# The first expert pair's rows: one-hot matrix held stationary, token rows streamed 512 columns at a time

## The chip, the cores and the metric

The kernel runs on one core of a Trainium2 chip, in one launch. The metric is device time in microseconds (us). Before the change, three runs gave 748.46, 750.91 and 753.99 us; the median is 750.91 us. Lower is better. The trace comes from one further, profiled execution of the same kernel.

## The reference

The reference is one decoder layer on 512 tokens of 1024 float32 values. Only its second half matters here, a hierarchical mixture of experts:

```python
hn2 = rms_norm(h, ffn_norm_g[l]).reshape(Bsz * S, D)
...
g_idx = jnp.argmax(p_group, axis=-1)                      # one of 4 groups per token
top_vals, top_idx = lax.top_k(logits_sel, TOP_K)          # two of its 8 experts
...
act = jax.nn.silu(hg) * hu * comb[:, g, :, None]
y = y + jnp.einsum('tef,efd->td', act, w_down[g])
```

In the first half the layer does a short gated convolution, a differential attention and an output projection; the sum of these and the input is `h`. Every token then goes to 2 of 32 experts, each a SwiGLU network with two matrices of 1024x512 (gate, up) and one of 512x1024 (down), all float32. The reference computes every expert for every token and weights most of them with zero.

## The kernel before, in words

**Stages.** The kernel works through the input projection, convolution and attention, the output projection together with the routing, and then the experts two by two (16 pairs). The tensor `y` holds h in SBUF: 128 partitions (tokens) by 4 chunks by 1024 columns. Each expert has 64 slots, so that a pair fills 128 rows. Tokens beyond 64 for one expert are left to a loop at the end (`overflow`).

**Rows of a pair.** For every later pair q the kernel makes a one-hot matrix of tokens by slots (`prepare`, L939), gets the token number of each slot by a small product (`index`, tile `pi`, L948), and fetches the rows with an indirect DMA from a copy of h in DRAM (`hrow`) to the SBUF tile `xr`. `turned` (L996 and on) then turns these rows: eight TensorE transposes of 128x128 into two PSUM banks of four each (tile `pxt2`, L1003), which ScalarE (L1009, one bank, four instructions) and VectorE (L1006, the other bank, one instruction) scale by the norm's gain `gf` and write to `xt`. Each `xt[:, k]` is a stationary operand of the gate and up products (`gate_up`, L1018 and L1019); column k of eight is every eighth value of a row.

**Rows of the first pair.** For pair 0 no DMA is used. `first_slots` makes its one-hot matrix `oh0` chunk by chunk (L853), once `place` (L834) has the positions of the chunk's tokens. `first_rows(c, h)` (L856 to L862) then multiplies: for each of four k, 128 columns of `y` (every eighth one) are the stationary operand and `oh0[:, c]` is the moving one, so that the result comes out already turned, in PSUM tile `px[h]`. It accumulates over the four chunks c. `first_turned` (L980 to L986) scales `px[0]` with VectorE (L983) and `px[1]` with ScalarE (L985) into `xt`. The trace has two matmul records for each float32 product, so 4 chunks x 2 halves x 4 products are 64 records on L861.

**Order.** The schedule is by hand: each engine executes in the order in which the program issues. Around the change, TensorE's order is: output projection of chunk 3 (`po`), `first_rows(0, 0)`, transposes of chunk 3 for the router (`pht`, L688), positions of chunk 1 (`ppos`, L831), `first_rows(0, 1)`, router of chunk 3 (`pr`, L695), positions of chunk 2, `first_rows(1, 0)`, `(1, 1)`, `(2, 0)`, positions of chunk 3, `first_rows(2, 1)`, `(3, 0)`, `(3, 1)`, the index products of pair 1 (`pi`), the counts, and then the gate and up products of expert 0 (`pgu`). VectorE runs the router's selection of each chunk (`route`, L796 to L822, ending in `ohm`) between these. After expert 0's products TensorE gets the gates of pair 0 by a product (`pcw`, L991), which needs `comb`, the end of a chain of small VectorE and ScalarE instructions (`gates`).

**Weights.** SP's queue issues the expert weights in a fixed order (L740) into a ring of 8 tiles of 2 MB (`we`) and one of 4 tiles of 1 MB (`wm`); a load waits until the tile it overwrites has been used. ScalarE's queue writes `hrow` and the gates `crow` to DRAM; GpSimd's queue issues the indirect fetches into `xr` and `cw`.

**Memory.** `xr` has one buffer. Before the change it is first filled with zeros by GpSimd (L1146); pair 1's fetch then writes to it.

Of the kernel before, what the change touches and what calls it, by code (L numbers as in the profile page):

```python
# [8 lines left out]
F32 = mybir.dt.float32  # L9
# [4 lines left out]
AF = mybir.ActivationFunctionType  # L14
OP = mybir.AluOpType
AX = mybir.AxisListType

P = 128
D = 1024
S = 512  # L20
NT = S // P
KD = D // P
# [17 lines left out]
def layer(ctx: ExitStack, tc: tile.TileContext, x, attn_norm_g, w_in, conv_w, conv_out_g,  # L40
# [3 lines left out]
    V, A, T = nc.vector, nc.scalar, nc.tensor  # L44
# [8 lines left out]
    def bank(tag, name, shape=(P, 512)):  # L53
        return psum.tile(list(shape), F32, name=name, tag=tag, bufs=BANKS[tag])
# [4 lines left out]
    def bc(ap, n):  # L59
        return ap.to_broadcast(n)  # L60
# [62 lines left out]
    y = cons.tile([P, NT, D], F32, name="y")  # L123
    xr = x[0].rearrange("(c p) d -> p c d", p=P)
# [10 lines left out]
    G = nc.gpsimd  # L135
# [7 lines left out]
    gf = cons.tile([P, KD], F32, name="gf")  # L143
# [629 lines left out]
    def rtt(name, *shape, dt=F32, bufs=1):  # L773
        return rt.tile([P] + list(shape), dt, name=name, bufs=bufs)
# [74 lines left out]
    oh0 = rtt("oh0", NT, 2, SLOTS)  # L849
    px = []  # L850
# [4 lines left out]

    def first_rows(c, h):  # L856
        if len(px) == h:
            px.append(bank("S", "px", (P, 4, P)))
        for j in range(4):
            k = 4 * h + j  # L860
            T.matmul(px[h][:, j], y[:, c].rearrange("p (q k) -> p k q", k=KD)[:, k], oh0[:, c].rearrange("p n s -> p (n s)"),  # L861
                     start=(c == 0 and j == 0), stop=(c == NT - 1 and j == 3), skip_group_check=True)  # L862

    def placed(c):
        positions(c)
# [4 lines left out]
    for c in range(NT):  # L870
        out_rest(c, (5,))
        if c:
            router(c - 1, 1)
            advance(tails[c - 1], 4)
        out_rest(c, (6, 7))
        h_add(c, 1, ob[1][c])
        if c < NT - 1:
            out_rest(c + 1, (4,))
        else:
            first_rows(0, 0)  # L880
        h_transposed(c, 1)
        A.dma_start(hrow[c * P:(c + 1) * P, :], y[:, c])
        if c > 1:
            placed(c - 2)
        if c:
            advance(tails[c - 1], 50)
    first_rows(0, 1)
    router(NT - 1, 1)
    placed(NT - 2)
    advance(tails[3], 50)  # L890
    first_rows(1, 0)
    first_rows(1, 1)
    first_rows(2, 0)
# [6 lines left out]
    moe = ctx.enter_context(tc.tile_pool(name="moe", bufs=1, reuse_waits="tile"))  # L900
# [69 lines left out]
    def prepare(q, tag="X"):  # L970

        oh = one_hot(posm[:, :, 2 * q:2 * q + 2], 2)

        def rest():
            i = index(oh, vcol[:, q:q + 1], tag)
            rows[q], cws[q] = fetch(i, P)
            return lambda: fetch_gates(cws[q], i, P)
        return rest

    def first_turned():  # L980

        xt = moe.tile([P, KD, P], F32, name="xt", tag="xt")
        V.tensor_tensor(xt[:, 0:4], px[0], bc(gf[:, 0:4, None], [P, 4, P]), op=OP.mult)  # L983
        for j in range(4):
            A.activation(xt[:, 4 + j], px[1][:, j], AF.Copy, scale=gf[:, 4 + j:5 + j])  # L985
        return xt  # L986

    def first_gates():
        p = pcw
        for c in range(NT):  # L990
            T.matmul(p, oh0[:, c].rearrange("p n s -> p (n s)"), comb[:, c], start=(c == 0), stop=(c == NT - 1))  # L991
        cws[0] = moe.tile([P, NE + 2], F32, name="cw", tag="cw", bufs=3)
        V.tensor_copy(cws[0], p)
        V.tensor_copy(vcol[:, 0:1], p[:, NE + 1:])

    def turned(x, m, tag="X"):  # L996

        xt = moe.tile([P, KD, P], F32, name="xt", tag="xt")
        x = x.rearrange("s (q k) -> s k q", k=KD)
        for k2 in range(2):  # L1000
            p = bank(tag, "pxt2", (P, 4, P))
            for j in range(4):
                T.transpose(p[:, j, 0:m], x[0:m, 4 * k2 + j], idf[0:m, 0:m])  # L1003
            if k2:
                ks = slice(4 * k2, 4 * k2 + 4)
                V.tensor_tensor(xt[:, ks, 0:m], p[:, :, 0:m], bc(gf[:, ks, None], [P, 4, m]), op=OP.mult)  # L1006
            else:
                for j in range(4):
                    A.activation(xt[:, j, 0:m], p[:, j, 0:m], AF.Copy, scale=gf[:, j:j + 1])  # L1009
        return xt  # L1010

    def gate_up(wg, wu, x, h, p, between=None):
# [91 lines left out]
    def overflow(inc, n):  # L1104

        with tc.For_i(0, n, 1):
# [25 lines left out]
            V.tensor_mul(le[0:SLOTS], le[0:SLOTS], cw[0:SLOTS, 0:NE])  # L1132
            V.tensor_reduce(wcol[0:SLOTS], le[0:SLOTS], axis=AX.X, op=OP.add)
            xt = turned(x, SLOTS)
            p = bank("G", "pgu")
            gate_up(w[0], w[1], xt, 0, p)
# [6 lines left out]
                    combine(s, *r, SLOTS, c, cs)  # L1143
            nc.sync.dma_start(oc, y)

    G.memset(moe.tile([P, D], F32, name="xr", tag="xr"), 0.0)  # L1146
    for _ in range(3):
        G.memset(moe.tile([P, NE + 2], F32, name="cw", tag="cw", bufs=3), 0.0)
    xts = {0: first_turned()}
    rest = prepare(1, "T")  # L1150
    fetch1 = rest()
    for cc in range(NT):
# [37 lines left out]
    for q in range(PAIRS):  # L1190
        if q:
            aT = down_t(acts.pop(q - 1), P)
        expert(2 * q)
        if q + 2 < PAIRS:
            rest = prepare(q + 2)
        if q:
            down_pair(q - 1, aT)
        if q == LAST:
            expert(2 * q + 1, lambda: combine_all(q - 1))
        else:  # L1200
            expert(2 * q + 1)
        if q < LAST:
            xts[q + 1] = turned(rows.pop(q + 1), P)
        if q + 2 < PAIRS:
            rest()()
        if 0 < q < LAST:
            combine_all(q - 1)
        if q == 2:
            rt_cm.__exit__(None, None, None)
            lp = ctx.enter_context(tc.tile_pool(name="lp", bufs=1, side="right", reuse_waits="tile"))  # L1210
            nt = lp.tile([P, NE], F32, name="nt")
            inc = lp.tile([P, 2, NE], F32, name="inc")
            tot = lp.tile([P, 1], I32, name="tot")
            it = lp.tile([P, 1], F32, name="it")
            inc = overflow_count()
        if q == 4:
            more = nc.values_load(tot[0:1, 0:1], min_val=0, max_val=NE)
# [57 lines left out]
```

## Time and profile before

| what | value |
|---|---|
| runs | 748.46, 750.91, 753.99 us |
| profiled execution, its own time | 753.25 us |
| its span | 751.5 us |
| mean granted TensorE clock | 0.987 of full speed |
| PE (matmul) busy | 696.5 us, 93% of the span |
| PEld (weight load) busy | 397.6 us, 53% |
| DVE (VectorE) busy | 317.1 us, 42% |
| ACT (ScalarE) busy | 192.8 us, 26% |
| POOL (GpSimd) busy | 73.7 us, 10% |
| DMA moved | 229.41 MB, mean 305 GB/s |

The span is the time from the first to the last instruction of the profiled execution; its own time is 1.75 us longer. Busy shares are means over stages that differ. The page also has a row of DMA throughput in 40 equal slices: it lies near 425 GB/s from about 225 us to 715 us, with one low slice of 290 GB/s at 282 to 300 us. A wait for several things is put down to the one that came last.

### The profile page before, as it was taken

The numbers are of one execution on the slowest core, as the hardware profiler recorded it, in microseconds if no ns is written. First come the engines' busy times: TensorE is split into PE (matmuls) and PEld (weight loads), VectorE is DVE, ScalarE is ACT, GpSimd is POOL, SyncE is SP. The second block draws the span as 40 slices with busy tenths as digits, with TensorE's granted clock in tenths as the row PEclk, the third lists the DMA queues.
The fourth block names the chain that finished last, engine by engine and source line by source line (L and its number), as shares of the span: only waits on it lengthen the run. The fifth ranks groups of instructions, "written<-read, shape, count | busy, mean of one in ns | idle before, by whom it ended". The sixth has DMA issues, their size and how long they took to land.

```text
span 751.5 us, 8843 instructions
## 1 busy us (share of the span) xinstructions
PE 696.5 (93%) x3356; PEld 397.6 (53%) x3356; DVE 317.1 (42%) x646; ACT 192.8 (26%) x409; POOL 73.7 (10%) x100
## 2 busy tenths in 40 slices
PE   6998999999899999999999989998898998997984
PEld 4786778777778783434434424434344343342432
DVE  2465767776642552235414414414132242331332
ACT  2555545554334211111111111111111111110111
POOL 5021300211110011001101101101001010010001
PEclk9999999999999999999999999999998999999998
DMA  8231221122229997999999999999999999999963
GB/s 267 62 108 56 85 57 57 56 58 66 73 70 422 420 413 290 421 428 418 426 421 426 425 420 427 426 423 422 423 427 428 417 424 430 421 425 423 416 220 114
DMA packets 45933, 229.41 MB, mean 305 GB/s; under 512 B 5156, under 2 KB 22822, under 8 KB 31041
## 3 DMA queue, kind: packets, MB, share of 16 engines
q1 hardware_dynamic: 41072, 221.79, 72.7%
q0 software_dynamic: 3136, 4.35, 1.8%
q10 hardware_dynamic: 1680, 2.69, 1.0%
q8 instruction: 27, 0.44, 0.2%
q14 instruction: 18, 0.14, 0.1%
HBM read 228.63 MB, written 4.26 MB: 310 GB/s over the span
## 4 chain that ended last, share of the span: by engine, by line
PE 42%; DMA 34%; issue 11%; DVE 7%; ACT 3%; POOL 2%; SPq 0%; POOLq 0%; ACTq 0%
DMA we<-in_w_exp_gate_dram 11%; DMA we<-in_w_exp_down_dram 9%; PE pgu L1018 7%; DMA wm<-in_w_exp_gate_dram 5%; DMA we<-in_w_exp_up_dram 5%; PE pgu L1019 5%; DMA wm<-in_w_exp_up_dram 4%; PE pdn L1042 4%; PE pq L118 3%; PE pq L119 3%; PE pq L117 3%; PE px L861 2%; PE po L117 1%; PE po L119 1%; PE po L118 1%
## 5 line engine op out<-in xcount | busy, mean ns | idle before, releaser
L1019 PE MATMUL pgu<-we,xt 128*64 128x512 f32 x400 | 181.2, 606 | 17.1 <-DMA we<-in_w_exp_up_dram 17.1
L1018 PE MATMUL pgu<-we,xt 128*64 128x512 f32 x400 | 182.5, 606 | 0.3 <-DMA we<-in_w_exp_gate_dram 0.3
L1025 DVE SCALAR_TENSOR_TENSOR act<-act,cw,pgu 64x512 f32<-64x512 f32 x32 | 23.9, 747 | 213.6 <-ACT act L1024 213.6
L1042 PE MATMUL pdn<-we,aT 128*64 128x512 f32 x384 | 90.6, 594 | 5.8 <-DMA we<-in_w_exp_down_dram 5.8
L1019 PEld LDWEIGHTS pgu<-we,xt 128*64 128x64 f32 x400 | 53.9, 139 | 75.0 <-issue 50.7
L1018 PEld LDWEIGHTS pgu<-we,xt 128*64 128x64 f32 x400 | 53.8, 139 | 58.8 <-issue 56.1
L1024 ACT ACTIVATE act<-pgu,cw 64x512 f32<-64x512 f32 x32 | 21.9, 683 | 234.0 <-PE pgu L1019 190.4
L1080 DVE TENSOR_TENSOR y<-y,pcb 128x512 f32<-128x512 f32 (+1 forms) x129 | 76.9, 666 | 4.2 <-PE pcb L1077 4.0
L1042 PEld LDWEIGHTS pdn<-we,aT 128*64 128x64 f32 x384 | 28.6, 137 | 65.8 <-issue 54.6
L1060 DVE TENSOR_TENSOR rl<-pdn,rh 128x512 fp32r<-128x512 f32 (+1 forms) x33 | 22.3, 675 | 84.8 <-ACT rh L1059 83.1
L1076 PE MATMUL pcb<-rh,sel 128*128 128x512 f32 (+1 forms) x132 | 51.9, 395 | 0.0
L1077 PE MATMUL pcb<-rl,sel 128*128 128x512 f32 (+1 forms) x132 | 50.4, 384 | 0.0
L1019 PE MATMUL pgu<-wm,xt 128*64 128x512 f32 x112 | 49.5, 595 | 0.8 <-DMA wm<-in_w_exp_up_dram 0.8
L1018 PE MATMUL pgu<-wm,xt 128*64 128x512 f32 x112 | 49.8, 595 | 0.2 <-DVE vcol L951 0.2
L961 POOL DMA_INDIRECT xr<-hrow,idx x15 | 15.1, 1006 | 349.1 <-DVE vcol L951 336.9
L109 DVE TENSOR_TENSOR wlo<-raw,whi 128x1024 fp32r<-128x1024 f32 x30 | 37.7, 1255 | 22.7 <-ACT whi L102 22.7
L1059 ACT ACTIVATE rh<-pdn 128x512 fp32r<-128x512 f32 (+1 forms) x33 | 19.3, 584 | 101.5 <-PE pdn L1042 94.4
L117 PE MATMUL pq<-whi,xh 128*128 128x512 f32 x96 | 41.0, 427 | 3.5 <-ACT whi L102 2.0
L117 PE MATMUL pcv<-xh,whi 128*128 128x512 f32 x96 | 41.8, 435 | 0.0
L118 PE MATMUL pq<-wlo,xh 128*128 128x512 f32 x96 | 39.0, 406 | 0.5 <-DVE wlo L109 0.5
L119 PE MATMUL pq<-whi,xl 128*128 128x512 f32 x96 | 39.0, 406 | 0.0
L119 PE MATMUL pcv<-xh,wlo 128*128 128x512 f32 x96 | 38.1, 397 | 0.0
(243 smaller groups left out, 1023.1 us busy)
## 6 DMA issues: line engine op xcount, KB each, us to landing
we<-in_w_exp_gate_dram SPq DMA_DIRECT2D x24, 2048.0 KB, 19.3
we<-in_w_exp_up_dram SPq DMA_DIRECT2D x24, 2048.0 KB, 31.0
we<-in_w_exp_down_dram SPq DMA_DIRECT2D x24, 2048.0 KB, 33.3
wm<-in_w_exp_gate_dram SPq DMA_DIRECT2D x14, 1024.0 KB, 27.6
wm<-in_w_exp_up_dram SPq DMA_DIRECT2D x14, 1024.0 KB
raw<-in_w_in_dram SPq DMA_DIRECT2D x24, 512.0 KB, 3.7
wm<-in_w_exp_down_dram SPq DMA_DIRECT2D x12, 1024.0 KB, 33.5
raw<-in_w_out_dram SPq DMA_DIRECT2D x8, 512.0 KB, 3.6
```

The costliest lines, as they stand in the source:

```text
L109: V.tensor_sub(los[i], raws.pop(i), his[i].bitcast(F32))
L117: T.matmul(o, lh, rh, start=start, stop=False)
L118: T.matmul(o, lh, rl, start=False, stop=False)
L119: T.matmul(o, ll, rh, start=False, stop=stop)
L1018: T.matmul(p[HS[1 - h]], l, wg[k], start=(k == 0), stop=(k == KD - 1))
L1019: T.matmul(p[HS[h]], l, wu[k], start=(k == 0), stop=(k == KD - 1))
L1025: V.scalar_tensor_tensor(a, a, w, p[HS[h]], op0=OP.mult, op1=OP.mult)
L1042: T.matmul(p[hf][HS[h]], aT[:, c, HS[h]], ws2[h][c][:, HALF[hf]], start=(c == 0), stop=(c == 3))
L1060: V.tensor_sub(r[1][0:m, cs], p[0:m], r[0][0:m, cs].bitcast(F32))
L1076: T.matmul(p, s[0:m, ts], rh[0:m, cs], start=True, stop=False)
L1077: T.matmul(p, s[0:m, ts], rl[0:m, cs], start=False, stop=True)
L1080: V.tensor_add(ys, ys, p)
```

## The change

`first_rows` has the operands exchanged: `oh0[:, c]` (128 columns) is stationary and 512 contiguous columns of `y` move, so one product replaces four. The result `px[h]` is then rows by columns, not turned. So it is copied to `xr` (one half by ScalarE, one by VectorE), and the function `turned` that every later pair uses turns it, with PSUM banks of tag K and with the roles of the two engines exchanged (`on_scalar=1`: VectorE scales columns 0 to 3, ScalarE 4 to 7, as `first_turned` did). `first_turned` and the filling of `xr` with zeros go.

```diff
     def first_rows(c, h):
         if len(px) == h:
-            px.append(bank("S", "px", (P, 4, P)))
-        for j in range(4):
-            k = 4 * h + j
-            T.matmul(px[h][:, j], y[:, c].rearrange("p (q k) -> p k q", k=KD)[:, k], oh0[:, c].rearrange("p n s -> p (n s)"),
-                     start=(c == 0 and j == 0), stop=(c == NT - 1 and j == 3), skip_group_check=True)
+            px.append(bank("S", "px"))
+        T.matmul(px[h], oh0[:, c].rearrange("p n s -> p (n s)"), y[:, c, 512 * h:512 * h + 512],
+                 start=(c == 0), stop=(c == NT - 1))
...
-    def first_turned():
-
-        xt = moe.tile([P, KD, P], F32, name="xt", tag="xt")
-        V.tensor_tensor(xt[:, 0:4], px[0], bc(gf[:, 0:4, None], [P, 4, P]), op=OP.mult)
-        for j in range(4):
-            A.activation(xt[:, 4 + j], px[1][:, j], AF.Copy, scale=gf[:, 4 + j:5 + j])
-        return xt
...
-    def turned(x, m, tag="X"):
+    def turned(x, m, tag="X", on_scalar=0):
...
-            if k2:
+            if k2 != on_scalar:
                 ks = slice(4 * k2, 4 * k2 + 4)
                 V.tensor_tensor(xt[:, ks, 0:m], p[:, :, 0:m], bc(gf[:, ks, None], [P, 4, m]), op=OP.mult)
             else:
                 for j in range(4):
-                    A.activation(xt[:, j, 0:m], p[:, j, 0:m], AF.Copy, scale=gf[:, j:j + 1])
+                    k = 4 * k2 + j
+                    A.activation(xt[:, k, 0:m], p[:, j, 0:m], AF.Copy, scale=gf[:, k:k + 1])
...
-    G.memset(moe.tile([P, D], F32, name="xr", tag="xr"), 0.0)
     for _ in range(3):
         G.memset(moe.tile([P, NE + 2], F32, name="cw", tag="cw", bufs=3), 0.0)
-    xts = {0: first_turned()}
+    xr = moe.tile([P, D], F32, name="xr", tag="xr")
+    A.activation(xr[:, 0:512], px[0], AF.Copy)
+    V.tensor_copy(xr[:, 512:D], px[1])
+    xts = {0: turned(xr, P, "K", 1)}
```

## Rows read from the trace of the kernel before

**Rows 1.** Busy time by stretch: PE, PEld, DVE, ACT, POOL; clock, DMA share, GB/s

```profile
224.00:280.00 56.00, 54.79 (x294) 46.15 (x294) 24.58 (x88) 14.62 (x33) 2.27 (x5) 1.00 1.00 417
280.00:285.00 5.00, 5.00 (x26) 1.50 (x22) 2.35 (x16) 1.59 (x3) 0.00 (x0) 1.00 0.73 221
...
293.00:299.00 6.00, 5.57 (x34) 2.90 (x34) 1.58 (x4) 2.42 (x6) 1.49 (x2) 1.00 0.46 129
299.00:715.00 416.00, 392.18 (x1840) 167.36 (x1836) 136.55 (x258) 61.97 (x129) 27.47 (x28) 0.99 1.01 423
```

**Rows 2.** Timeline of SP's queue: start, duration, engine, line, load

```profile
258.52 0.85 SPq L740 DMA_DIRECT2D wm<-in_w_exp_up_dram  x2
...
281.83 0.81 SPq L740 DMA_DIRECT2D wm<-in_w_exp_gate_dram  x2
...
296.49 0.80 SPq L740 DMA_DIRECT2D we<-in_w_exp_down_dram  x2
```

**Rows 3.** Waits of SP's queue, 281 to 284 and 290 to 300: total, times, longest

```profile
SPq L740 <- PE pgu L1019: 10.3, 1, 10.3
...
SPq L740 <- DMA crow<-comb: 10.3, 1, 10.3
```

**Rows 4.** Chain of waits from 255 to 290: start, duration, engine, tile, line

```profile
260.67 1.78 PE px L861 x8
262.45 0.44 PE pht L688 x4
...
262.97 0.20 DVE posm L834
...
265.88 0.18 PE ppos L831
...
271.95 5.80 PE px L861 x24
...
278.15 0.64 PE pgu L1018
```

**Rows 5.** Chain of waits of the whole span: two operations found elsewhere

```profile
206.04 0.87 PE pcn L426 x2
...
316.36 1.09 PE pxt L1003 x8
```

**Rows 6.** Timeline of VectorE, 255 to 296

```profile
260.95 0.68 DVE L674 TENSOR_TENSOR y<-y,po 128x512 f32<-128x512 f32 x1
...
266.53 0.15 DVE L796 TENSOR_REDUCE rm<-pr 128x1 f32<-128x4 f32 x1
...
269.63 0.25 DVE L822 SCALAR_TENSOR_TENSOR ohm<-w,rm,oh 128x32 bf16<-128x32 f32 x1
...
275.89 0.69 DVE L983 TENSOR_TENSOR xt<-px,gf 128x512 f32<-128x512 f32 x1 [3.37 <-PE px L861]
276.50 0.68 DVE L939 TENSOR_TENSOR oh<-slots,posm 128x512 f16<-128x512 f32 x1
```

**Rows 7.** Timeline of ScalarE and its DMA queue, 255 to 296

```profile
261.73 0.63 ACT L676 ACTIVATE hsq<-y 128x512 f32<-128x512 f32 x1 [3.77 <-DVE y L674]
...
282.80 0.38 ACTq L927 DMA_DIRECT2D crow<-comb  x1
```

**Rows 8.** ScalarE's groups to 300 us: count, busy, mean ns, idle before

```profile
L690 ACT ACTIVATE hT<-pht 128x512 f32<-128x512 f32 x8 | 4.8, 596 | 8.8 <-PE pht L688 8.3 <-PE ppos L831 0.5
```

**Rows 9.** Timeline of TensorE just ahead of expert 0

```profile
277.59 0.24 PE L948 MATMUL pi<-tok,oh 128*128 128x1 f16 x4
```

**Rows 10.** Busy time by stretch, after two idle gaps of TensorE

```profile
444.00:450.00 6.00, 6.00 (x22) 1.83 (x24) 0.00 (x0) 0.00 (x0) 0.00 (x0) 0.72 1.03 426
730.00:736.00 6.00, 6.00 (x36) 2.87 (x33) 1.16 (x3) 0.98 (x2) 0.00 (x0) 1.00 0.00 0
```

**Rows 11.** Timeline of TensorE: the two gaps, in brackets, and their releasers

```profile
443.95 0.64 PE L1019 MATMUL pgu<-we,xt 128*64 128x512 f32 x1 [2.84 <-DMA we<-in_w_exp_up_dram]
...
728.19 0.75 PE L1031 MATMUL pat<-idf,act 128*128 128x128 f32 x4 [1.57 <-DVE act L1025]
```

## The prediction

> **What bounds the kernel now.** I first read busy time by stretch. From 299 to 715 us the DMA engines are full (share 1.01, 423 GB/s) while TensorE has 24 us to spare of 416: here the weight stream sets the pace, and the end comes when the stream ends. Before that, from 224 to 280, both are full (417 GB/s, and PE busy 54.79 of 56), and between them the stream breaks off twice: 221 GB/s from 280 to 285 and 129 GB/s from 293 to 299 [rows 1]. The reader is to see that an early gain of TensorE's is worth only what it moves these two breaks. Against 423 GB/s they lost 5 x (1 - 221/423) = 2.4 us and 6 x (1 - 129/423) = 4.2 us, 6.6 in all: more than that can't be won here.
>
> Next, what ends the breaks, in SP's queue and its waits. The first ends with loads at 281.83, which waited for expert 0's gate and up products to free a tile; the second with loads at 296.49, which waited last for the landing of the gates' write to DRAM, `crow` [rows 2, 3]. That write is issued at 282.80 [rows 7], after the gates' chain, which starts when the last rows of pair 1's index have been read; expert 0's products start there too. So if expert 0 starts d earlier, both breaks end about d earlier, and the stream, with nothing else to slow it, ends d earlier.
>
> Last, what sets the start of expert 0, at 278.15: the chain of waits runs through the 64 records of the first rows (24 of them take 5.80 us, 0.242 each), broken by the route of chunk 2 on VectorE [rows 4].
>
> **The change, part by part.** All new times are estimates on the trace's clock.
>
> *Products.* 64 records x 0.242 = 15.5 us go. Eight products of 128 stationary and 512 moving columns in float32 come; the one like them in the trace, `pcn`, takes 0.87 us for its two records [rows 5]: 8 x 0.87 = 7.0. TensorE has 8.5 us less to do. Not all of it shortens the path, because VectorE's routes are late next:
> - `first_rows(0, 0)` runs from 260.67 to 261.54. The transposes `pht` need the sum `y`, done at 260.95 + 0.68 = 261.63 [rows 6]; they start at 261.67 and not 262.45. `posm` follows 0.52 later as it does now [rows 4], at 262.19, 0.78 earlier.
> - From `posm` to `ppos` of chunk 2 it is 265.88 - 262.97 = 2.91, all VectorE's route; so `ppos` at 265.10. TensorE meanwhile does `(0, 1)` until 263.0 and the router, whose transposed input ScalarE delivers after its squares (261.73 + 0.63 and the read of the sum) and a copy of 0.60 [rows 7, 8], at about 263.1. Done by 263.9, it idles 1.2 us.
> - Three products: 265.28 + 2.61 = 267.89. The route of chunk 3 starts 0.65 after `ppos` and takes 269.88 - 266.53 = 3.35 [rows 6]: from 265.75 to 269.10. TensorE idles 1.2 us again, does `ppos`, and from 269.23 the last three products, until 271.84. The one-hot of chunk 3 is ready at about 269.9, before `(3, 0)` wants it at 270.1.
>
> Products end at 271.84 and not 271.95 + 5.80 = 277.75: 5.9 us earlier; the other 2.6 of the 8.5 are idle time.
>
> *Copies, turning, scaling.* Before, `px[0]` was scaled beside the last products, and only 0.4 us lay between the last product and expert 0. Now they are in series. ScalarE's copy of `px[0]` lies beside the last product. VectorE's copy of `px[1]` is not in the trace in this form; VectorE's scaling from PSUM of the same shape takes 0.69 [rows 6], and ScalarE's plain copy 0.60 [rows 8]. Bounds 0.5 and 0.8; I take 0.69, the same engine: 271.88 to 272.57. All eight transposes wait for both copies, since each takes every eighth column. From 272.61 they take 1.09 for eight [rows 5]; their first bank is ready near 273.30 (four transposes and the drain). VectorE scales it from 273.32, ScalarE the second beside that. The next VectorE instruction, pair 1's one-hot, starts 0.61 after the scaling and takes 0.68 [rows 6]: it ends at 274.61. The index products follow at 274.65, and expert 0 follows them by 278.15 - 277.59 = 0.56, as now [rows 4, 9]: **275.21**, 2.9 us earlier. ScalarE's scaling ends by 275.0; expert 0 wants it only at its fifth k.
>
> The transposes stand at the trace's 0.136 us each. The Trainium skill ("TensorE: Matmul & The Clock Gate", Part 4: PE-mode transpose) gives about 275 ns for one in a kernel and says that the full clock doesn't engage for them; by its figure eight would take 2.2 us, an estimate, and the gain would be 1.8. The trace disagrees: 1.09 for eight, and a granted clock of 1.00 in the stretch from 293 to 299, which holds eight [rows 1].
>
> *Zeros of `xr`.* They lie on GpSimd, with nothing waiting; cost nothing. Pair 1's fetch into `xr` now also waits for the eight transposes, which end a microsecond before its index is there: nothing. ScalarE's copy waits ahead of the gates' chain in its queue, but that chain needs VectorE's later counts anyway: nothing.
>
> *Weights for expert 0.* Their last loads are issued at 258.52 [rows 2]. What was sent from 224 up to and including them is 16.8 MB and 2.1 MB of `hrow`; at 417 GB/s [rows 1] this has landed by about 270, five microseconds before the new start.
>
> *Carried on.* First break: SP's loads at 278.9, before the backlog ends near 280, so the break closes and 4.2 MB keep the stream full until about 290. Second break: `crow` is issued at 279.9; before, it landed just ahead of 296.49 [rows 2], 13.7 us after its issue, the last 3 of them beside a nearly empty stream [rows 1]. Counted from its issue or from the end of the weights, it lands at about 293.6, and the stream resumes 2.9 earlier.
>
> **Sum.** -2.9 us. The profiled execution took 753.25 for a span of 751.5, 2.3 over the median of the runs shown. It becomes 750.3; the median 750.91 becomes **748.0**.
>
> **The rivals.**
> 1. *Forecast*, 748.0: own range 746 to 750, from the copy, the idle steps and `crow`. Chance 0.64.
> 2. *The gain stops at `crow`.* Its write lands no earlier, because it is now sent beside a full stream and not in the first break. For: its landing and not TensorE ends the longest wait. Against: the weights ahead of it run out at 290, and before it needed only 3 us beyond that point. Gain 0 to 1: 750 to 751. Chance 0.16.
> 3. *Both breaks close.* `crow` lands with its issue, unhindered, and SP goes on when expert 1 frees its tile; bounded by 6.6 us: 744.3. Against: nothing moves that tile by more than 2.9, so at most the 3 us that `crow` lagged are added, near 745. Chance 0.07.
> 4. *Slower: the clock falls.* TensorE is idle twice for 1.2 us and then about 0.8 and 0.9, between short work. The trace has a gap of 2.84 us after which the granted clock was 0.72 over six microseconds (partly the lower level, 1.2 GHz), and one of 1.57 with 1.00 after it [rows 10, 11]. Place: from 267.9 on. At 1.2 GHz three products cost 2.6 more, the transposes 1.1, and expert 0 loses what that stretch lost, 6 x 0.28 = 1.7: 5.4. It decides once it costs more than 2.9: 748.0 + 5.4 = 753.4. Against: each gap is shorter than 1.57. Chance 0.06.
> 5. *The change doesn't do what it says*: a product of 512 moving columns costs as much as four old ones, 1.94. Then TensorE ends with the old 277.75, and the chain of 3.4 in place of 0.4 makes it 753.9. Against: `pcn`. Chance 0.03; unnamed mishaps 0.04.
>
> **How the numbers follow.** The likeliest case gives 748.0. The range takes case 2 and most of 3, and the runs' own spread of 748.46 to 753.99, which the median of a few runs still shows by a microsecond or so: 745.0 to 751.5, leaving out cases 4 and 5 and the edges. About 1% (7.5 us) is what a measurement of this kernel can tell from no change. No case reaches it: faster would need more than the breaks hold, slower more than cases 4 and 5 cost. Faster 0.03, same 0.94, slower 0.03.
>
> **What would show it.** In the changed trace: 16 records on `px`, 0.43 apart; TensorE idle ahead of `ppos` of chunks 2 and 3; the last product near 272; `pxt2` near 272.6; expert 0 near 275.2; SP's loads near 278.9 and 293.6; a full stream between 280 and 290. A late `crow` or a clock under 1.00 between 265 and 285 would speak for 2 or 4; `ppos` without a wait would make the route's part wrong.

## The result and the profile after

The changed kernel takes **746.76 us** (median of 12 runs, 745.43 to 748.54), the kernel before 751.31 (12 runs): ratio 0.9935, 95% interval 0.9921 to 0.995. That is 4.9 us less, between 3.8 and 5.9; the forecast was 748.0 and 2.9 less. The profiled execution of the changed kernel has a span of 745.3 and took 747.16.

Two executions differ before they reach the change: VectorE's sum `y` of chunk 3, which nothing in the diff touches, starts at 260.95 in the trace of before [rows 6] and at 259.03 in that of after. So I count from that sum. A time of after plus 1.92 is a time on the clock of before.

Busy time by stretch, after (PE, PEld, DVE, ACT, POOL; clock, DMA share, GB/s):

```profile
224.00:280.00 56.00, 50.75 (x266) 34.57 (x266) 25.95 (x101) 15.90 (x35) 1.37 (x4) 1.00 1.01 423
280.00:285.00 5.00, 5.00 (x30) 2.15 (x28) 1.60 (x4) 0.69 (x1) 0.00 (x0) 1.00 1.02 417
285.00:293.00 8.00, 7.57 (x46) 3.40 (x44) 1.57 (x4) 2.42 (x6) 0.64 (x1) 1.00 0.98 376
293.00:299.00 6.00, 6.00 (x32) 2.00 (x30) 0.00 (x0) 0.00 (x0) 2.38 (x3) 1.00 1.00 423
```

Against [rows 1] both breaks of the stream are gone: 417 where 221 stood, 423 where 129 stood. The same stretches counted from `y` (15 to 24, 24 to 32, 32 to 40 us after it), before and then after:

```profile
275.95:284.95 9.00, 8.79 (x48) 4.09 (x47) 4.74 (x26) 3.04 (x9) 1.13 (x1) 1.00 0.86 316
284.95:292.95 8.00, 8.00 (x42) 3.18 (x40) 1.60 (x4) 0.69 (x1) 0.00 (x0) 1.00 1.02 412
292.95:300.95 8.00, 7.57 (x44) 3.62 (x44) 1.58 (x4) 2.42 (x6) 3.03 (x3) 1.00 0.58 196
```

```profile
274.03:283.03 9.00, 9.00 (x46) 3.46 (x44) 3.38 (x23) 2.69 (x6) 1.13 (x1) 1.00 1.00 413
283.03:291.03 8.00, 7.57 (x44) 3.37 (x40) 2.56 (x4) 1.82 (x5) 0.00 (x0) 1.00 1.02 393
291.03:299.03 8.00, 8.00 (x41) 2.74 (x41) 0.29 (x3) 0.62 (x2) 3.02 (x3) 1.00 0.97 405
```

Added up from 37.5 us ahead of `y` to 60 behind it, before had moved 37.938 MB and after 40.178. At 423 GB/s that is a **lead of 5.3 us** for the weight stream, where the prediction had 2.9. Below, "lead" is this number for each kernel. It is still there at the end: the last `pat`, the transposes ahead of the last down products, starts 728.19 - 260.95 = 467.24 after `y` in before [rows 11] and 720.42 - 259.03 = 461.39 in after, 5.85 earlier.

The start of expert 0. TensorE's timeline of after, from the last rows' products to expert 0 (in brackets: idle time ahead, and its releaser):

```profile
259.77 0.66 PE L688 MATMUL pht<-idf,y 128*128 128x128 f32 x4
...
263.42 0.18 PE L831 MATMUL ppos<-ohm,tri 128*128 128x32 bf16 x1 [1.06 <-DVE ohm L822]
263.45 2.82 PE L859 MATMUL px<-y,oh 128*128 128x512 f32 x6
...
267.46 0.18 PE L831 MATMUL ppos<-ohm,tri 128*128 128x32 bf16 x1 [1.12 <-DVE ohm L822]
267.48 2.82 PE L859 MATMUL px<-y,oh 128*128 128x512 f32 x6
271.18 1.13 PE L993 MATMUL pxt<-idf,xr 128*128 128x128 f32 x8 [0.88 <-DVE xr L1141]
273.25 0.25 PE L946 MATMUL pi<-tok,oh 128*128 128x1 f16 x4 [0.94 <-DVE oh L937]
...
273.81 0.64 PE L1009 MATMUL pgu<-wm,xt 128*64 128x512 f32 x1 [0.20 <-DVE vcol L949]
```

VectorE in after, where the new copy and the scaling stand in series with these:

```profile
259.03 0.68 DVE L674 TENSOR_TENSOR y<-y,po 128x512 f32<-128x512 f32 x1
260.50 0.19 DVE L834 SCALAR_TENSOR_TENSOR posm<-ppos,ohm 128x32 f32<-128x32 f32 x1 [0.79 <-PE ppos L831]
...
270.34 0.69 DVE L1141 COPY xr<-px 128x512 f32<-128x512 f32 x1 [2.15 <-PE px L859]
271.90 0.69 DVE L996 TENSOR_TENSOR xt<-pxt,gf 128x512 f32<-128x512 f32 x1 [0.86 <-PE pxt L993]
272.51 0.68 DVE L937 TENSOR_TENSOR oh<-slots,posm 128x512 f16<-128x512 f32 x1
```

Expert 0 starts 14.78 after `y`; before, 278.15 [rows 4] - 260.95 = 17.20. So it starts **2.42 earlier**, in the way the prediction said: two idle stretches for VectorE's routes, then copy, transposes, scaling, one-hot and index one after the other.

SP's queue in after, and what it waited for between 284 and 300:

```profile
277.49 0.80 SPq L740 DMA_DIRECT2D wm<-in_w_exp_gate_dram  x2
280.93 0.80 SPq L740 DMA_DIRECT2D wm<-in_w_exp_up_dram  x2
288.95 3.01 SPq L740 DMA_DIRECT2D we<-in_w_exp_down_dram  x2
```

```profile
SPq L740 <- PE pgu L1010: 13.6, 2, 7.3
SPq L740 <- DMA crow<-comb: 2.3, 1, 2.3
```

Before, both down loads went out at 296.49, 35.54 after `y`, and the wait for `crow` was 10.3 long [rows 2, 3]. Now the first of the two goes out 29.92 after `y`, 5.62 earlier, released by TensorE; only the second waits for `crow`. `crow` itself did what was predicted. GpSimd's fetch that reads it, before; then after, its issue on ScalarE's queue (before's is in [rows 7]) and the fetch:

```profile
297.21 1.03 POOL L966 DMA_INDIRECT cw<-crow,idx  x1 [17.21 <-DMA crow<-comb]
```

```profile
278.15 0.38 ACTq L925 DMA_DIRECT2D crow<-comb  x1
```

```profile
292.36 1.03 POOL L964 DMA_INDIRECT cw<-crow,idx  x1 [16.70 <-DMA crow<-comb]
```

From issue to fetch 14.41 before and 14.21 after: counted from `y` the write lands 2.9 earlier. Its queue row is only 0.38 long. The Trainium skill ("Perfetto Trace Analysis", section on the HWDGE DMA instruction) says that such a row ends when the queue is free, while the completion comes when the write is confirmed, late above all for a write to HBM. These rows agree that the row ends long before the completion, 0.38 against some 14; what takes the 14 us no run shows.

So why does the first down load no longer wait for `crow`? The built programs' lists of waits tell it. A semaphore is a counter that a transfer raises when it is complete, and on which others wait. SP's loads and ScalarE's writes take eight of them in turn, DMAHW0 to DMAHW7, and a transfer waits for the last one that used its semaphore. The lines that differ around `crow`:

```
before   crow <- comb     waits DMAHW2, VectorE
         wm <- up         waits DMAHW3, TensorE
         we <- down (1st) waits DMAHW2, TensorE
         we <- down (2nd) waits TensorE
after    crow <- comb     waits DMAHW3, VectorE
         wm <- up         waits DMAHW2, TensorE
         we <- down (1st) waits TensorE
         we <- down (2nd) waits DMAHW3, TensorE
```

In before, `crow` holds the semaphore that the first down load takes next, so the load waits for a write that has nothing to do with its tile. The edit moved `crow` to the second load's semaphore. Nothing in the diff names a semaphore: in the built program of before `crow` stands ahead of one of SP's loads, in that of after behind it, and so it takes the next place in the rotation.

One thing went against this execution. The last pair's `pdn` in after, behind two pauses of TensorE, and the granted clock there; before's `pat` with the same first pause is in [rows 11]:

```profile
720.42 0.74 PE L1022 MATMUL pat<-idf,act 128*128 128x128 f32 x4 [1.57 <-DVE act L1016]
721.91 7.08 PE L1043 MATMUL pdn<-we,aT 128*64 128x512 f32 x32 [0.75 <-ACT aT L1024]
```

```profile
721.00:723.00 2.00, 1.25 (x6) 0.44 (x6) 0.00 (x0) 0.60 (x1) 0.00 (x0) 0.80 0.00 0
723.00:725.00 2.00, 2.00 (x6) 0.49 (x4) 0.00 (x0) 0.00 (x0) 0.00 (x0) 0.50 0.00 0
```

Before:

```profile
729.69 5.38 PE L1052 MATMUL pdn<-we,aT 128*64 128x512 f32 x32 [0.75 <-ACT aT L1033]
```

The clock fell to 0.50, which is 1.2 GHz, and the 32 records took 7.08 instead of 5.38: 1.70 lost in this execution. The same fall is seen below with the products of before (e1), so it does not need the change.

### The profile page after: what moved, and what is told of

Same layout as the page of the kernel before. It is cut to its first block, busy times and chain, and to the rows that moved or that the text cites. A ratio compares the mean times of both kernels' runs of the same rounds, so it can differ in the third digit from the quotient of the medians.

```text
span 745.3 us, 8763 instructions
## 1 busy us (share of the span) xinstructions
PE 691.9 (93%) x3316; PEld 389.7 (52%) x3316; DVE 317.7 (43%) x647; ACT 193.2 (26%) x410; POOL 72.6 (10%) x99
## 3 DMA queue, kind: packets, MB, share of 16 engines
q10 hardware_dynamic: 1680, 2.69, 1.0%
## 4 chain that ended last, share of the span: by engine, by line
PE 50%; DMA 32%; DVE 8%; issue 4%; ACT 3%; POOL 2%; SPq 0%; POOLq 0%; ACTq 0%
DMA we<-in_w_exp_up_dram 13%; DMA we<-in_w_exp_down_dram 9%; PE pgu L1009 9%; PE pgu L1010 7%; PE pdn L1033 6%; DMA we<-in_w_exp_gate_dram 5%; DMA wm<-in_w_exp_down_dram 4%; PE pq L118 3%; PE pq L119 3%; PE pq L117 3%; PE pcb L1067 2%; PE pcb L1068 2%; PE pcv L117 1%; PE pcv L119 1%; PE pcv L118 1%
## 5 line engine op out<-in xcount | busy, mean ns | idle before, releaser
L1033 PE MATMUL pdn<-we,aT 128*64 128x512 f32 x384 | 92.1, 613 | 6.0 <-DMA we<-in_w_exp_down_dram 5.8
L1050 ACT ACTIVATE rh<-pdn 128x512 fp32r<-128x512 f32 (+1 forms) x33 | 19.3, 584 | 105.7 <-PE pdn L1033 96.9
```

Source lines behind the costliest of these rows:

```text
L1033: T.matmul(p[hf][HS[h]], aT[:, c, HS[h]], ws2[h][c][:, HALF[hf]], start=(c == 0), stop=(c == 3))
```

## The experiments

All runs in one table. "Start" is expert 0's first `pgu` record after `y`, "load" SP's first down load after `y`, "gap" their difference; "sem" is the load that shares `crow`'s semaphore (1st, 2nd, or none where GpSimd's queue writes it). Lead as above. "pdn" is the last group of 32. A ratio goes against runs of the kernel before on the same chip; the times come from several chips, so that ratios are what to compare.

| kernel | time | ratio (95%) | start | load | gap | sem | lead | pdn |
|---|---|---|---|---|---|---|---|---|
| before | 751.31 | | 17.20 | 35.54 | 18.34 | 1st | 0 | 5.38 |
| after | 746.76 | 0.9935 (0.9921-0.995) | 14.78 | 29.92 | 15.14 | 2nd | 5.3 | 7.08 |
| e1 | 749.94 | 0.9973 (0.9961-0.9985) | 17.20 | 32.34 | 15.14 | none | 3.0 | 7.08 |
| e2 | 750.26 | 0.9979 (0.9966-0.9991) | 17.20 | 32.34 | 15.14 | 2nd | 2.8 | 5.38 |
| e3 | 751.58 | 0.9994 (0.9978-1.0009) | 17.20 | 35.59 | 18.39 | 1st | -0.2 | 5.38 |
| e4 | 747.85 | 0.9947 (0.9929-0.9965) | 16.23 | 31.37 | 15.14 | 2nd | 3.7 | 5.38 |
| e5 | 747.64 | 0.9948 (0.993-0.9965) | 13.39 | 31.84 | 18.45 | 1st | 3.6 | 5.38 |
| e6 | 746.5 | 0.9938 (0.9917-0.996) | 13.61 | 28.75 | 15.14 | 2nd | 6.1 | 5.38 |
| e7 | 747.81 | 0.9954 (0.9938-0.997) | 14.79 | 29.93 | 15.14 | none | 5.3 | 7.08 |
| e8 | 747.59 | 0.9948 (0.9929-0.9967) | 13.63 | 28.77 | 15.14 | none | 5.9 | 7.08 |
| e9 | 748.25 | 0.9952 (0.9936-0.9968) | 12.43 | 31.70 | 19.27 | 1st | 3.7 | 5.38 |
| e10 | 746.5 | 0.9932 (0.9913-0.9951) | 14.79 | 29.93 | 15.14 | 2nd | 5.4 | 5.38 |
| e11 | 745.78 (one run) | | 14.79 | 29.92 | 15.13 | 2nd | 5.5 | 5.38 |
| e12 | 745.94 | 0.9924 (0.991-0.9937) | 13.62 | 28.76 | 15.14 | none | 5.9 | 5.38 |

The column to read first is the gap. Wherever `crow` is off the first load's semaphore it is 15.13 or 15.14, whatever else was changed: that load goes out when expert 1 is done with its tile. Wherever `crow` is on it, the gap is 18.3 to 19.3.

**The semaphore alone, in the kernel before (e1, e2, e3).** e1 issues `crow` from GpSimd's queue; nothing else in the program's text differs.

```diff
-        A.dma_start(crow.rearrange("(c p) e -> p c e", p=P), comb)
+        G.dma_start(crow.rearrange("(c p) e -> p c e", p=P), comb)
```

> The kernel before, with one edit: the write of crow is issued from GpSimd's queue and not from ScalarE's, so that it no longer shares a completion semaphore with SP's loads. Theory L (semaphore): in the kernel before, the first load of the two down matrices after expert 1 had to wait for crow's landing only because both used the same semaphore; so that load now goes out when expert 1 frees its tile, near 293.2 and not 296.49, the break of 293 to 299 shrinks from 4.2 us lost to about 1, and the time falls by 2.5 to 3.3 us, to about 748.3, with the products untouched. Rival S (start): the end follows the start of expert 0 alone, which does not move here: within 0.5 us of before.

e2 keeps the write on ScalarE's queue and puts ten tiny copies on ScalarE ahead of it, which pushes `crow` one place on in the rotation, to the second load's semaphore; e3 puts six there, which leaves the semaphores as they were, so it shows what the copies alone do.

```diff
+        for _ in range(10):
+            A.activation(eg4, eg4, AF.Copy)
         A.dma_start(crow.rearrange("(c p) e -> p c e", p=P), comb)
```

> The kernel before, with ten tiny ScalarE copies ahead of the write of crow, so that crow is issued 1 to 2 us later; in the built program crow then has the semaphore of the second down load, as in the changed kernel, and the first down load waits for TensorE alone. Theory L: although crow is later, the first down load goes out near 293.2; the second waits for crow until about 298, but 2 MB bridge some 5 us: 2 to 3 us faster than before, about 748.8. Rival S: crow later can only hurt: 0 to 1.5 us slower, 751 to 753.

> Control for the run with ten copies: six copies, crow about 1 us later, and the semaphores as in the kernel before (the first down load waits for crow). Theory L: the first down load goes out about 1 us later than 296.49, the time is 0.5 to 1.2 us more than before, about 752. Rival S: 0 to 1 us more.

SP's waits between 284 and 300, of e2 and then of e3:

```profile
SPq L740 <- PE pgu L1021: 7.3, 1, 7.3
SPq L740 <- DMA crow<-comb: 3.6, 1, 3.6
```

```profile
SPq L740 <- DMA crow<-comb: 10.3, 1, 10.3
SPq L740 <- PE pgu L1021: 2.6, 1, 2.6
```

In e2 `crow` is issued 281.90 - 258.42 = 23.48 after `y`, 1.63 later than before, and yet the load goes out 3.2 earlier. Expert 0's start is untouched in all three. e1 and e2 gain 2.0 us (1.1 to 2.9) and 1.6 (0.7 to 2.6) and their streams 3.0 and 2.8; e3 gains nothing. The times gain less than the 2.5 to 3.3 and 2 to 3 that were expected, and e3 isn't the 0.5 to 1.2 slower either: its `crow` is issued 0.65 later after `y`, and the load goes out only 0.05 later.

e1 alone would leave a rival: from GpSimd's queue the write also lands sooner, 290.01 - 281.63 = 8.38 from its issue to the fetch, which is ahead of the load at 291.85. e2 leaves none, since its `crow` is issued later than before's. With e3 beside it the semaphore is shown to be a cause by itself, worth about 2.9 us of stream and some 2 of time.

**The start alone, in the kernel after (e4).** Three idle products ahead of the copies delay expert 0.

```diff
+    pd = bank("O", "pdum")
+    for n in range(3):
+        T.matmul(pd, oh0[:, 3].rearrange("p n s -> p (n s)"), y[:, 3, 512:D], start=True, stop=True)
     xr = moe.tile([P, D], F32, name="xr", tag="xr")
```

> The changed kernel with three more products of 512 columns into an unused bank ahead of the turning of the first rows, so that expert 0 starts about 2.6 us later, near where it started in the kernel before; semaphores as in the changed kernel (the second down load waits for crow). Theory L: the part of the gain that comes from the semaphore stays: 2 to 2.5 us faster than before, about 749, the first down load near 293 on the clock of the kernel before. Rival S: the gain is gone, within 0.5 us of before.

The delay came out at 1.45 and not the 2.6 that was expected. Start and load both move by it, the lead falls by 1.6, and the ratio rises by 0.0012, some 0.9 us (the intervals overlap). So while the tile and not `crow` releases the load, the stream follows a later start nearly one for one. An earlier start brings less, near the 6.6 us that the breaks hold: e6 and e8 below start 1.17 and 1.15 earlier than after and lead by 0.8 and 0.6 more.

**Start against semaphore (e5, e6).** Both leave out the copies and the turning, so that the first pair gets rows that are not turned; two idle products (their result is read by nobody) give back part of the time. e6 has one more idle product, of 128 columns, and with it the rotation falls the other way.

```diff
-    A.activation(xr[:, 0:512], px[0], AF.Copy)
-    V.tensor_copy(xr[:, 512:D], px[1])
-    xts = {0: turned(xr, P, "K", 1)}
...
+    pd = bank("O", "pdum")
+    for n in range(2):
+        T.matmul(pd, oh0[:, 3].rearrange("p n s -> p (n s)"), y[:, 3, 512:D], start=True, stop=True)
+    V.tensor_tensor(xts[0][:, 0:4], px[0].rearrange("p (j s) -> p j s", j=4), bc(gf[:, 0:4, None], [P, 4, P]), op=OP.mult)
...
```

> The changed kernel without the copies and without the turning: the new products are scaled straight into the stationary tile, so the first pair is fed rows that are not turned and its part of the output is not the reference's; two idle products of 512 columns stand ahead of expert 0 so that it starts about 1.3 us earlier than in the changed kernel, 3.7 us earlier than before. In the built program crow shares its semaphore with the first down load, as before. Theory L (semaphore): the first down load waits for crow until 13.7 us after its issue, about 3 us after expert 1 has freed the tile; 1 to 1.5 us slower than the changed kernel's own stream would be, total 747 to 748. Rival S (start): 3.7 us faster than before, 748, or better than the changed kernel by 1.3.

> The same as the run with two idle products, with one more idle product of 128 columns (0.2 us of TensorE); in the built program crow now has the semaphore of the second down load, as in the changed kernel. So the two runs differ by 0.2 us of start, against this one, and by the semaphore. Theory L: 2 to 3 us faster than the other, 745.5, with the first down load when expert 1 frees its tile. Rival S: 0.2 us slower than the other, no difference that can be measured.

SP's waits between 284 and 300, of e5 and then of e6:

```profile
SPq L740 <- DMA crow<-comb: 10.5, 1, 10.5
SPq L740 <- PE pgu L1010: 5.2, 1, 5.2
```

```profile
SPq L740 <- PE pgu L1010: 13.0, 2, 7.2
SPq L740 <- DMA crow<-comb: 2.9, 1, 2.9
```

e5 starts expert 0 1.39 earlier than after does, and its load goes out 1.92 later; its lead is 3.6 against 5.3. e6 starts 0.22 later than e5 and is 2.5 us of stream ahead of it. Between the ratios the intervals overlap, but both contain the spread of the same runs of before. Taken against each other, on one chip, seven of e5's eight times lie above all six of e6's (medians 747.64 and 746.5): the time shows the difference too, some 1.1 us where 2 to 3 were expected.

**Is `crow`'s queue worth anything more (e7)?** After, with e1's edit.

> The changed kernel with the write of crow issued from GpSimd's queue: no down load waits for crow. Theory L: the second down load no longer waits its 2.3 us, but the stream was kept busy by the first, so only what is still lost between 280 and 300 us is to be had: 0 to 1 us faster than the changed kernel, about 746.3. Rival S: the same as the changed kernel, 746.8.

Start, load and lead are those of after. The wait that is left, 2.3 us on the second load, costs the stream nothing; the first load's 2 MB, some 5 us at 423 GB/s, cover it. The time, 747.81, is above both values that were expected, 746.3 and 746.8; the interval of its ratio overlaps that of after.

**What made the old products dear (e9)?** Before, with 128 neighbouring columns of `y` as the stationary operand, so that the first pair's rows come in another order.

```diff
-            T.matmul(px[h][:, j], y[:, c].rearrange("p (q k) -> p k q", k=KD)[:, k], oh0[:, c].rearrange("p n s -> p (n s)"),
+            T.matmul(px[h][:, j], y[:, c, k * P:(k + 1) * P], oh0[:, c].rearrange("p n s -> p (n s)"),
```

> The kernel before, with one edit: the stationary operand of the old products is 128 neighbouring columns of y in place of every eighth column (the rows are then fed in another order, which leaves that part of the computation changed). It asks what made the old products dear. Theory S (the stride of the stationary operand did): their weight loads fall from 0.33 us to about 0.14 to 0.19 and a record on px from 0.242 to about 0.126, as pcw's in the trace of before; the last 24 take about 3.0 instead of 5.80, expert 0 then starts 12.5 to 14 after the sum y instead of 17.2, and with no turning at all the kernel is 3 to 4.5 us faster than before (about 747.5). Rival M (the count of instructions, or 128 moving columns, did): the pace stays at 0.24 and the time at before's, within 0.7 us.

Weight loads by line (count, then busy and mean ns), before and then e9:

```profile
L861 PEld LDWEIGHTS px<-oh,y 128*128 128x128 f32 x64 | 15.5, 333 | 0.2 <-issue 0.2
```

```profile
L861 PEld LDWEIGHTS px<-oh,y 128*128 128x128 f32 x64 | 7.5, 192 | 2.3 <-issue 2.2
```

TensorE's timeline of e9, the last 24 records and expert 0:

```profile
267.24 2.92 PE L861 MATMUL px<-oh,y 128*128 128x128 f32 x24
270.65 0.25 PE L948 MATMUL pi<-tok,oh 128*128 128x1 f16 x4 [0.49 <-DVE oh L939]
...
271.22 0.64 PE L1018 MATMUL pgu<-wm,xt 128*64 128x512 f32 x1 [0.20 <-DVE vcol L951]
```

The last 24 records take 2.92, against 5.80 in [rows 4]; the six of after that do the same work take 2.82. So it was the stride of eight, in the stationary operand, and not the number of products: four neighbouring 128-column products cost 8 x 2.92/24 = 0.97, one of 512 columns 2.82/3 = 0.94. The Trainium skill ("SBUF — State Buffer", Door 1) has SBUF lines of 16 bytes, and a penalty for each access that goes to a new one; a step of eight float32 is 32 bytes, and 333 against 192 ns agrees. Expert 0 starts 4.77 earlier, twice what the change brings, but the load waits for `crow` (gap 19.27), and the lead, 3.7, ends below that of after. The ratios, 0.9952 and 0.9935, have intervals that overlap.

**The clock at the end (e10, e11).** e11 is the changed kernel once more; e10 fills the pauses around the last `pat` with idle products.

```diff
+    pw = bank("X", "pwarm")
+    for n in (512, 192):
+        T.matmul(pw[:, 0:n], idf, y[:, 0, 0:n], start=True, stop=True)
...
+    for n in (256,):
+        T.matmul(pw[:, 0:n], idf, y[:, 0, 0:n], start=True, stop=True)
```

> The changed kernel once more, nothing edited, for a second profile of it. If the fall of the clock ahead of the last pdn group belongs to the program, the group takes 7.08 us again; if it belongs to the execution, 5.38 may be seen, and the span less the time of the sum y is then about 1.7 us shorter than in the first profile of it (486.3), near 484.6. Expert 0 starts 14.8 after y, and SP's first load for the next tile 29.9 after y, in both cases.

> The changed kernel, with idle TensorE products of 512 and 192 columns ahead of the last pair's turning and 256 columns behind it, so that the two pauses of 1.57 and 0.75 us are filled; their results are read by nobody. Theory C (these pauses let the granted clock fall in some executions, and the last 32 records of pdn then take 7.08 instead of 5.38): the last pdn group takes 5.38, and the median falls by 0 to 1.7 us, as many executions as fall; about 746. Rival (the fall does not hang on the pauses but on the executions, the chip's or the die's state): 7.08 may be seen again here, and the time stays at 746.8 within 0.6.

TensorE at the end, e11 and then e10:

```profile
720.67 0.74 PE L1022 MATMUL pat<-idf,act 128*128 128x128 f32 x4 [1.57 <-DVE act L1016]
722.16 5.38 PE L1043 MATMUL pdn<-we,aT 128*64 128x512 f32 x32 [0.75 <-ACT aT L1024]
```

```profile
719.87 1.45 PE L1214 MATMUL pwarm<-y,idf 128*128 128x512 f32 x4
721.52 0.75 PE L1022 MATMUL pat<-idf,act 128*128 128x128 f32 x4 [0.19 <-DVE act L1016]
722.10 0.60 PE L1217 MATMUL pwarm<-y,idf 128*128 128x256 f32 x2
723.01 5.38 PE L1043 MATMUL pdn<-we,aT 128*64 128x512 f32 x32 [0.31 <-ACT aT L1024]
```

The same program with the same two pauses took 7.08 once and 5.38 once: the fall belongs to the execution. Of the twelve profiles with these pauses four show it (after, e1, e7, e8); the two without them don't. But eight of twelve with them don't either, and e10's time, 0.9932, is that of after, 0.9935. Whether the pauses are needed for the fall is open. So is whether the change makes it likelier: of the profiles with both pauses, one of five with the old order of operands fell (e1) and three of seven with the new one. A hint on the timed runs is their mean granted clock over the whole span: 0.980 in the four profiles that fell and 0.981 to 0.991 in the ten others. It is 0.980 or less in 5 of after's 12 runs and in 13 of the 59 runs of before that were taken beside the experiments, so the medians of both kernels may hold such falls.

**Put together (e8, e12).** e8 is e7 with pair 1's one-hot and index ahead of the copies and the turning, e12 is e8 with the idle products of e10.

```diff
+    rest = prepare(1, "T")
     A.activation(xr[:, 0:512], px[0], AF.Copy)
     V.tensor_copy(xr[:, 512:D], px[1])
+    fetch1 = rest()
     xts = {0: turned(xr, P, "K", 1)}
-    rest = prepare(1, "T")
-    fetch1 = rest()
```

> The changed kernel with crow on GpSimd's queue and with pair 1's one-hot and index taken ahead of the turning, so that they lie beside the copies: expert 0 starts about 1.2 us earlier. If the weight stream is what is left (theory L), it can gain no more than the 1 us the stream still loses around 285 to 293: 745.5 to 746.8. If TensorE's start still sets the end (rival S), 1.2 us less than the changed kernel: 745.6. The two differ in the bytes moved: under L the stream's lead grows by less than the start's.

> The changed kernel with three edits together: pair 1's index work ahead of the copies and the turning (which starts expert 0 1.2 us earlier), the gates' write on GpSimd's queue (which keeps it off the loads' semaphores), and the idle products at the end. If the three are worth what their steps say, the stream's lead over before is 5.9 us as with the first two alone, the last pdn group takes 5.38, and the time is 745 to 746, about 1 under the changed kernel. Rival (the two first bring nothing that the end shows, as their run without the third said, and the clock falls whatever is done): 747.0 to 747.8.

The hoist starts expert 0 1.15 earlier and adds 0.6 to the lead. e8's time, 747.59, shows none of it and is above both values that were expected (745.5 to 746.8, and 745.6); e12's, 745.94, is the lowest median of the timed kernels, but its interval overlaps that of after, so it is not shown to be better.

## Why the prediction was right or wrong

**The bound: right.** The stream sets the end, and an early gain counts by what it moves the two breaks; of the 6.6 us that they could give, 5.3 came, and the last `pat` starts 5.85 earlier, 5.27 in e11.

**The products and the idle time: right.** 2.69 of chain for the last six records against 3 x 0.87; idle 1.06 and 1.12 against 1.2 twice.

**Copies and turning: right.** VectorE's copy took the 0.69 that was borrowed from its scaling, and the eight transposes 1.13 against 1.09, at a granted clock of 1.00 up to 299. That again is not the 275 ns each (a figure for bf16), without the full clock, of the Trainium skill ("TensorE: Matmul & The Clock Gate", Part 4).

**The start: 275.73 on the clock of before, against 275.21.** Of the half microsecond, 0.21 is `posm`, which follows `pht` by 0.73 and not 0.52; the rest is some 0.15 in products and 0.1 in the handover to the transposes. Weights and zeros cost nothing that shows: what expert 0 waited for last was `vcol`.

**The first break: right.** SP's loads at 277.49 + 1.92 = 279.4, against 278.9, and 417 GB/s behind them.

**The second break: the step that failed, though the time lay in the range.** Of `crow` it was said: "it lands at about 293.6, and the stream resumes 2.9 earlier." The first half held: from `y`, the fetch of `crow` came 2.9 earlier, beside a full stream, which also ends rival 2. The second half did not: the load went out 5.6 earlier. I took the wait for `crow` in [rows 3] for a property of the stage, where it was one of the built program's choice of semaphore. The load's tile has no use for `crow`; that question, asked of the wait, would have shown a condition that an edit elsewhere can flip. Rival 3 had the price right ("at most the 3 us that `crow` lagged", against 18.34 - 15.14 = 3.2) and half of its condition (SP goes on when expert 1 frees its tile), but asked for a `crow` that lands sooner as well, and so had a chance of 0.07.

**The clock: rival 4 did not come where it was placed**, between 267.9 and 285 the granted clock is 1.00. The clock fell at the end instead, in some executions, in e1 too, which has before's products.

**The sum.** In the profiled executions: start 2.42, semaphore 2.87 (the rest of the lead 5.29; e1 and e2 give 3.0 and 2.8 for it alone), clock at the end -1.70: 3.6. Counted from `y`, the span fell by (751.5 - 260.95) - (745.3 - 259.03) = 4.28. The 0.7 that is left over arose on the way: the last `pat` is 5.85 ahead and not 5.3, and from it to the end after takes 745.3 - 720.42 = 24.88 and before 751.5 - 728.19 = 23.31, 1.57 more. A lead taken 60 us behind `y` thus holds to about a microsecond at the end (e2: 2.8 there, 1.65 at the last `pat`). For e11, where the clock stayed, the span fell by (751.5 - 260.95) - (744.0 - 258.70) = 5.25 for a lead of 5.5. The medians' 4.55 lies between the two.

**Right for part of the reason.** The start gave 2.42 of the 2.9 that were forecast, and the rest of the gain came from a semaphore that the prediction did not see. The time, 746.76, is 1.2 under the forecast and in the range because the range took in most of rival 3, which had the second break closed for another reason; that part is luck. The gain was missed by more, 4.55 against 2.9; the difference, 0.4, is that the median of before, 750.91 from three runs, is 751.31 with twelve. That a loss at the end took part of the gain back is shown for the profiled execution alone.

## What to carry to other kernels

When a transfer waits for another that shares no data with it, look in the built program for the semaphore that they share: the wait can come or go with edits that touch neither transfer (ten tiny copies in e2, one idle product in e6), and it belongs in the forecast as a case of its own. Before counting instructions of a costly group, look at the stride of its stationary operand. A start that comes earlier is worth only what the next release in the queue lets through: e9's 4.77 us gave a lead of 3.7, the changed kernel's 2.42 one of 5.3.

## What was not expected of the hardware

- A weight load of 128x128 float32 took 333 ns with a step of eight columns and 192 without, in the same place of the same kernel (e9).
- A write of 512 rows of 34 float32 took about 14 us from its issue on ScalarE's queue to the fetch that waited for it, beside a full weight stream and beside an interrupted one alike (14.21 and 14.41). Issued from GpSimd's queue, the same write took 7.7 to 8.7 (e1, e7, e8, e12); no run shows why.
- The granted clock fell to 0.50 behind pauses of 1.57 and 0.75 us in four of twelve profiles, two executions of one program among them differing; why is open.
